# Log-sum-exp over heads on one core: 4 MB loads in place of 2 MB, bias parts taken as single rows by the first units, and factors made at the start of the late stages

## The chip, the cores and the metric

The kernel runs on one core of a Trainium2 chip. The metric is the device time of one execution in microseconds (us); the median of three executions of the kernel before is 326.98 us (326.78 to 327.11).

## The reference

`x` has 8 batches of 2048 rows with 2048 columns in float32; `bias` has 8 heads of 256 columns. Each row of `x` is cut into 8 heads, the head's bias is added, and the logarithm of the sum of exponentials is taken over the 256 columns. Every result is then written twice, for two neighbouring output rows.

```
x_heads = x.reshape(B, S, H, Dh).transpose(0, 2, 1, 3) + bias[None, :, None, :]
x_tiled = np.repeat(x_heads, 2, axis=2)
mx = x_tiled.max(axis=-1, keepdims=True)
lse = mx.squeeze(-1) + np.log(np.exp(x_tiled - mx).sum(axis=-1))
```

The kernel does without the maximum. It reads 134 MB of `x` and writes 1 MB.

## The kernel before

**Tiling.** A unit `t` is 256 rows of one batch: 128 partitions with K = 2 rows each, 2 MB. There are T = 64 units, eight to a batch. Nine buffers `xt` of 2 MB take them in turn (`NBUF = 9`). In the first seven batches a partition holds two neighbouring rows, one run of 16 KB in memory. The last batch (from unit 56) is laid out with consecutive rows on consecutive partitions. From unit 57 on a unit is loaded and worked on as single rows per partition (1 MB, `K` pieces), and unit 63 in still smaller pieces of columns (`LAST_COLS`). Below, (57,0) is the first row per partition of unit 57.

**The stages.** `STAGES` gives a split of the eight heads over the engines, by unit.

- Units 0 to 53 (`BULK`): heads 0 to 2 get their bias on the tensor engine (PE): three matmuls put the bias into PSUM (`put_bias`, L216), three more add `x` through an identity (`late_heads`, L275). The scalar engine (ACT) takes exp out of PSUM: head 0 with a running sum (L286), heads 1 and 2 back into the buffer (L293). Heads 4 to 7 get the bias from GpSimd (POOL) in place (`g_add`, L325). Then ACT takes exp of heads 3 to 7 (`later`, L331), the vector engine (DVE) multiplies head 3 by exp(bias) (L343) and adds up heads 1 to 7 in one reduction (L350).
- Units 54 to 56 (`MIXED`): head 0 goes over PE and ACT (`add_x` L251, `sum_biased` L306), heads 1 to 3 are exponentiated raw and weighed with exp(bias) on DVE (`weigh`, L366), heads 4 to 7 as in the bulk.
- From unit 57 on: single rows; POOL has no addition any more but folds one or two heads (`fold`, L382 and L390, with the rest on DVE at L396), DVE weighs the others.

**Factors and bias parts.** exp(bias) stands in `one_ps` (heads 1 and 2, PSUM), `w_ps` (heads 3 to 6, PSUM) and `w_sb` (heads 6 and 7). `one_ps` serves head 0 of the bulk as well, so its factors are made when unit 54 begins, behind unit 54's products on PE (`spread` L182, exp L500). The bias itself enters PE as three bfloat16 parts that add up to it: POOL makes them on one partition (`bparts`, L172 to L176), and three DMAs from POOL's queue put them on three partitions (`b3`, L178), so that one matmul with three rows adds all three.

**The order.** The program fixes the order by hand (`tc.manual_schedule`). In unit t's turn PE takes its products, POOL its addition, ACT and DVE do what was put off from unit t-1 (`for_pool`: exp of POOL's heads, the reduction), then ACT the heads of t. [...] The load of unit t + 9 is issued on SyncE's queue (SP, L143) after unit t's last step in program order, and waits for the last reads of the buffer. `on_x` keeps a list of who has touched a buffer, and drops those waits that follow from others.

**Results.** The sums of a batch stand in `R` (128 partitions x 2 rows x 8 heads x 8 blocks). `finish`, two units after a batch's end, turns them with two transposes on PE (L411) and takes Ln on ACT (L421, 64 partitions x 512). After unit 57 `store` writes seven batches at once (L425). `finish_last` does the same for the last batch (L432, L438, L439).

```
def load(t):
    after = last_uses[t - NBUF] if t >= NBUF else []
    for k0, k1, c0, c1 in pieces(t):
        loads[t, k0, c0] = on_x(t, nc.sync.dma_start(
            out=xts[t % NBUF][:, k0:k1, c0:c1], in_=rows_of(t)[:, k0:k1, c0:c1]), after)
```

Of the kernel before, what the change touches and what calls it, by code (L numbers as in the profile page):

```python
# [9 lines left out]
F32 = mybir.dt.float32  # L10
BF16 = mybir.dt.bfloat16
ACT = mybir.ActivationFunctionType
ALU = mybir.AluOpType


K = 2
NBUF = 9

NWARM = 3

# [29 lines left out]
def kernel(  # L50
# [6 lines left out]
    nc = tc.nc  # L57
    P = nc.NUM_PARTITIONS
    B, S, D = x.shape
    H, Dh = bias.shape  # L60
    assert D == H * Dh and S % (P * K) == 0
    NBLK = S // (P * K)
    T = B * NBLK
# [12 lines left out]
    brow = sb.tile([1, D], F32, name="brow")  # L76
    b_rep = sb.tile([P, D - G0], F32, name="b_rep")
    w_sb = sb.tile([P, D - W1], F32, name="w_sb")
    ident = sb.tile([P, P], F32, name="ident")
    ones = sb.tile([1, P], F32, name="ones")  # L80
    ones3 = sb.tile([3, P], BF16, name="ones3")
    b3 = sb.tile([3, CPE], BF16, name="b3")
    bparts = sb.tile([1, 3, CPE], BF16, name="bparts")
    brest = sb.tile([1, 2, CPE], F32, name="brest")

    R = [sb.tile([P, K, H, NBLK], F32, name=f"R{b}") for b in range(B - 1)]
    R_last = sb.tile([P, H, NBLK, K], F32, name="R_last")
    res = sb.tile([H * NBLK, B - 1, P, K, 2], F32, name="res")
    res_last = sb.tile([P, P, 2], F32, name="res_last")
    xts = [sb.tile([P, K, D], F32, name=f"xt{i}") for i in range(NBUF)]  # L90
    w_ps = pp.tile([P, W2 - W0], F32, name="w_ps")


    one_ps = pp.tile([P, MM], F32, name="one_ps")
    pairs = [pp.tile([P, 2 * MM], F32, name=f"pair{i}") for i in range(2)]
    ps = [p[:, c : c + MM] for p in pairs for c in (0, MM)]
    tpair = pp.tile([P, 2, K, P], F32, name="tpair")
    tps = [tpair[:, i] for i in range(2)]

    def modes_of(t):  # L100
        return [modes for t0, modes in STAGES if t0 <= t][-1]
# [1 line left out]
    def pieces(t):  # L103

        if len(modes_of(t)) == 1:
            return [(0, K, 0, D)]
        cols = [[(0, D)]] * K if t < T - 1 else LAST_COLS
        return [(k, k + 1, c0, c1) for k in range(K) for c0, c1 in cols[k]]

    def rows_of(t):  # L110

        b, blk = divmod(t, NBLK)
        v = x[b, blk * P * K : (blk + 1) * P * K, :]
        if b < B - 1:
            return v.rearrange("(p k) d -> p k d", k=K)
        return v.rearrange("(k p) d -> p k d", k=K)

    users = [[] for _ in range(T)]  # L120

    def on_x(t, ins, after):
        known = [u for u in users[t] if u.ins.engine != ins.ins.engine]
        for before in range(t % NBUF, t, NBUF):
            known += users[before]
        for u in known:
            if u not in after:
                tc.declare_no_dep(
                    ins.ins, u.ins, reason="waited for by those it waits for"
                )  # L130
        users[t].append(ins)
        return ins

    loads = {}

    last_uses = [[] for _ in range(T)]

    def load(t):
        after = last_uses[t - NBUF] if t >= NBUF else []
        for k0, k1, c0, c1 in pieces(t):  # L140
            loads[t, k0, c0] = on_x(
                t,
                nc.sync.dma_start(  # L143
                    out=xts[t % NBUF][:, k0:k1, c0:c1],
                    in_=rows_of(t)[:, k0:k1, c0:c1],
                ),
                after,
            )

    order = tc.manual_schedule()  # L150
    order.__enter__()
# [55 lines left out]
    def put_bias(m, k0, k1):  # L207

        if m["late"]:
            pair = pairs[n_ps[0] % 2]
            n_ps[0] += 1
            got = [one_ps, pair[:, 0:MM], pair[:, MM : 2 * MM]]
            for h, p in enumerate(got):
                nc.tensor.matmul(  # L216
                    p,
                    lhsT=ones3,
                    rhs=each_row(b3, h * Dh, Dh, K),
                    start=True,  # L220
                    stop=False,
                )
            return got + [pair]
        n = m["pe"] * Dh
        rows = min(k1 - k0, max(MM // n, 1))
        got = []
        for k in range(k0, k1, rows):
            for c in range(0, n, MM):
                w = min(n - c, MM)
                bank = n_ps[0] % len(ps)  # L230
                p = ps[bank][:, 0 : rows * w]
                n_ps[0] += 1
                mm = nc.tensor.matmul(
                    p,
                    lhsT=ones3,
                    rhs=each_row(b3, c, w, rows),
                    start=True,
                    stop=False,
                )
                on_bank(bank, mm)  # L240
                got.append((k, k + rows, c, w, bank, p))
        return got

    def add_x(m, t, k0, c0, c1, got):
# [3 lines left out]
        for ka, kb, c, w, bank, p in got:  # L248
            if not c0 <= c < c1:
# [14 lines left out]
    def keep_warm():  # L264
        for _ in range(NWARM):
            nc.tensor.matmul(  # L266
                tps[B % 2][:, 0], lhsT=ident, rhs=ident, start=True, stop=True
            )

    def late_heads(m, t, got, sums):  # L270
# [134 lines left out]

    def finish(b):

        nr = H * NBLK
        tp = tps[b % 2]
        for k in range(K):  # L410
            nc.tensor.transpose(  # L411
                out=tp[0:nr, k],
                in_=R[b][:, k].rearrange("p h n -> p (h n)"),
                identity=ident,
            )
        tv = bass.AP(
            tensor=tp.tensor,
            offset=tp.offset,
            ap=[[tp.ap[0][0], nr], [1, P], [P, K], [0, 2]],
        )  # L420
        nc.scalar.activation(out=res[:, b], in_=tv, func=ACT.Ln)  # L421

    def store():

        nc.sync.dma_start(  # L425
            out=out[0 : B - 1].rearrange("b h (n r) -> (h n) b r", n=NBLK),
            in_=res.rearrange("q b p k r -> q b (p k r)"),
        )

    def finish_last():  # L430
        tp = tps[(B - 1) % 2][:, 0]
        nc.tensor.transpose(  # L432
            out=tp, in_=R_last.rearrange("p h n k -> p (h n k)"), identity=ident
        )
        tv = bass.AP(
            tensor=tp.tensor, offset=tp.offset, ap=[tp.ap[0], [1, P], [0, 2]]
        )
        nc.scalar.activation(out=res_last, in_=tv, func=ACT.Ln)  # L438
        nc.sync.dma_start(  # L439
            out=out[B - 1].rearrange("h (n r) -> (h n) r", r=2 * P),  # L440
            in_=res_last.rearrange("q p r -> q (p r)"),
        )


    def sums_of(t):

        b, blk = divmod(t, NBLK)
        if b < B - 1:
            return R[b][:, :, :, blk]
        return R_last[:, :, blk, :].rearrange("p h k -> p k h")  # L450


# [6 lines left out]
        (modes_of(t)[k0], k0, k1)  # L459
        for t in range(T)  # L460
        for k0, k1, c0, _ in pieces(t)
# [9 lines left out]
    for t in range(T):  # L471
        xt = xts[t % NBUF]
        sums = sums_of(t)
        for k0, k1, c0, c1 in pieces(t):
# [62 lines left out]
        fb, at = divmod(t - 2, NBLK)  # L537
# [39 lines left out]
```

## Time and profile before

| what | value |
|---|---|
| median of three executions | 326.98 us |
| the profiled execution's own time | 327.16 us |
| its span in the trace | 325.4 us |
| granted tensor clock, mean of the span | 0.921 |
| PE busy | 263.2 us (81%) |
| DVE busy | 284.0 us (87%) |
| ACT busy | 264.7 us (81%) |
| POOL busy | 290.7 us (89%) |
| read from memory, mean rate | 134.23 MB, 416 GB/s |
| POOL's additions, L325 | 57, 4543 ns each |
| DVE's reductions in the bulk, L350 | 3.89 us each |

One execution was profiled; its times come from that execution. An idle time in square brackets is that of the engine just before the instruction, with what ended it. "x2" behind a shape merges neighbouring instructions of one line. In the table of stretches the columns are: the stretch, its length, the engine's busy time and number of instructions, the granted tensor clock, the DMA engines' share, and GB/s. In the slices of the span each digit or number stands for 8.1 us.

### The profile page before, as it was taken

The page shows a single profiled execution, that of the slowest core. Times are in us where ns is not written, and L with a number is a line of the kernel's source. Part 1 is how long each engine was busy: PE and PEld are TensorE (multiplying, and loading weights), DVE is VectorE, ACT ScalarE, POOL GpSimd, SP SyncE. Part 2 cuts the span into 40 slices and gives each one's busy share as a digit, 9 for nine tenths or more (in the row PEclk, how much of TensorE's full clock was granted, in tenths as well). Part 3 has the DMA queues.
Part 4 walks back from the last instruction along what each step waited for, and adds up shares of the span by engine and source line. Part 5 has one row for each costly group of instructions (what it writes and reads, how often), then busy time and mean ns, then how long its engine had stood idle before and what let it go on. Part 6 is the DMA issues. An engine that isn't in the chain of part 4 may idle for free.

```text
span 325.4 us, 2350 instructions
## 1 busy us (share of the span) xinstructions
PE 263.2 (81%) x649; PEld 98.6 (30%) x649; DVE 284.0 (87%) x306; ACT 264.7 (81%) x425; POOL 290.7 (89%) x123
## 2 busy tenths in 40 slices
PE   5398999599888789779779788887877897399984
PEld 2033333233323223223223223323223332044442
DVE  1008999999999999998998899989899799999985
ACT  1139999499969878987887969698788778889995
POOL 7999999899999999999999999999999899958874
PEclk9999999899979987997997979798998989569999
DMA  7999999999999999999999999999999999999995
GB/s 293 428 435 429 427 433 422 425 433 429 427 427 431 425 424 433 425 425 434 426 425 431 431 422 427 429 429 427 431 427 426 429 425 429 415 421 421 424 394 154
DMA packets 11934, 135.42 MB, mean 416 GB/s; under 512 B 1361, under 2 KB 1745, under 8 KB 2961
## 3 DMA queue, kind: packets, MB, share of 16 engines
q1 hardware_dynamic: 11824, 135.27, 98.9%
q8 instruction: 5, 0.08, 0.1%
q14 instruction: 7, 0.06, 0.0%
q0 software_dynamic: 96, 0.00, 0.0%
q10 hardware_dynamic: 2, 0.01, 0.0%
HBM read 134.23 MB, written 1.05 MB: 416 GB/s over the span
## 4 chain that ended last, share of the span: by engine, by line
DMA 48%; DVE 35%; POOL 6%; ACT 6%; PE 3%; issue 1%; SPq 0%; DVEq 0%
DMA xt<-in_x_dram 45%; DVE R L350 29%; ACT xt L331 5%; DVE xt L343 5%; POOL xt L325 4%; DMA b<-bparts 2%; PE pair L275 2%; DVE xt L366 2%; PE one_ps L275 1%; ACT xt L293 1%; DMA brow<-in_bias_dram 1%; POOL brest L173 1%; POOL brest L175 1%; PE pair L216 0%; POOL bparts L172 0%
## 5 line engine op out<-in xcount | busy, mean ns | idle before, releaser
L325 POOL TENSOR_TENSOR xt<-xt,b_rep 128x2048 f32<-128x2048 f32 x57 | 258.8, 4543 | 20.1 <-DMA xt<-in_x_dram 20.1
L350 DVE TENSOR_REDUCE R<-xt 128x14 f32<-128x3584 f32 (+1 forms) x56 | 214.5, 3831 | 1.9
L331 ACT ACTIVATE xt<-xt 128x2560 f32<-128x2560 f32 (+5 forms) x77 | 158.1, 2062 | 13.4 <-POOL xt L325 12.5
L275 PE MATMUL pair<-xt,ident 128*128 128x512 f32 x216 | 115.1, 660 | 0.0
L275 PE MATMUL one_ps<-xt,ident 128*128 128x512 f32 x108 | 66.7, 702 | 23.1 <-DMA xt<-in_x_dram 23.1
L293 ACT ACTIVATE xt<-pair 128x1024 f32<-128x1024 f32 x54 | 56.3, 1042 | 20.7 <-PE pair L275 19.3
L275 PEld LDWEIGHTS pair<-xt,ident 128*128 128x128 f32 x216 | 46.2, 214 | 61.5 <-issue 61.5
L343 DVE TENSOR_TENSOR xt<-xt,w_ps 128x512 f32<-128x512 f32 x54 | 36.8, 681 | 27.8 <-ACT xt L331 27.7
L286 ACT ACTIVATE xt<-one_ps 128x256 f32<-128x256 f32 x108 | 40.6, 391 | 7.9 <-PE one_ps L275 7.9
L216 PE MATMUL one_ps<-b,ones 3*128 3x512 bf16 x54 | 20.7, 383 | 18.4 <-ACT xt L286 12.4
L216 PEld LDWEIGHTS <-ones 3*128 3x128 bf16 x162 | 13.5, 92 | 70.2 <-issue 63.8
L216 PE MATMUL pair<-b,ones 3*128 3x512 bf16 x108 | 32.3, 378 | 0.0
L275 PEld LDWEIGHTS one_ps<-xt,ident 128*128 128x128 f32 x108 | 17.0, 198 | 46.4 <-DMA xt<-in_x_dram 39.6
L251 PE MATMUL pair<-xt,ident 128*128 128x512 f32 (+1 forms) x36 | 21.0, 669 | 7.2 <-DMA xt<-in_x_dram 7.1
L286 ACT ACTIVATION_READ_ACCUMULATOR xt<-one_ps 128x1 f32 x108 | 23.5, 218 | 0.0
L366 DVE CUSTOM_DVE_ANT_0 xt<-xt,w_ps 128x256 f32<-128x256 f32 x61 | 22.4, 419 | 0.0
L390 POOL TENSOR_TENSOR xt<-xt 128x128 f32<-128x128 f32 (+3 forms) x39 | 13.9, 356 | 3.1
L382 POOL TENSOR_TENSOR xt<-xt,w_sb 128x256 f32<-128x256 f32 (+1 forms) x13 | 10.1, 773 | 5.4 <-ACT xt L331 4.8
L266 PE MATMUL tpair<-ident 128*128 128x128 f32 x84 | 13.6, 300 | 0.5 <-ACT res L421 0.5
L306 ACT ACTIVATE xt<-pair 128x256 f32<-128x256 f32 x33 | 12.3, 387 | 0.0
L266 PEld LDWEIGHTS tpair<-ident 128*128 128x128 f32 x84 | 11.1, 200 | 4.1 <-issue 3.0
L366 DVE CUSTOM_DVE_ANT_0 xt<-xt,one_ps 128x256 f32<-128x256 f32 x27 | 10.6, 416 | 0.7 <-ACT xt L331 0.7
(40 smaller groups left out, 68.5 us busy)
## 6 DMA issues: line engine op xcount, KB each, us to landing
xt<-in_x_dram SPq DMA_DIRECT2D x57, 2048.0 KB, 30.8
xt<-in_x_dram SPq DMA_DIRECT2D x12, 1024.0 KB, 24.7
xt<-in_x_dram SPq DMA_DIRECT2D x4, 256.0 KB, 11.4
out_dram<-res SPq DMA_DIRECT2D x1, 896.0 KB, 6.6
xt<-in_x_dram SPq DMA_DIRECT2D x2, 384.0 KB, 16.0
xt<-in_x_dram SPq DMA_DIRECT2D x2, 128.0 KB, 6.3
out_dram<-res_last SPq DMA_DIRECT2D x1, 128.0 KB, 1.7
b<-bparts POOLq DMA_DIRECT2D x3, 1.5 KB, 6.4
```

The source lines that it names most:

```text
L216: nc.tensor.matmul(p, lhsT=ones3, rhs=each_row(b3, h * Dh, Dh, K), start=True, stop=False,)
L251: mm = nc.tensor.matmul(p, lhsT=ident, rhs=xts[t % NBUF][:, ka:kb, c : c + w], start=False, stop=True,)
L266: nc.tensor.matmul(tps[B % 2][:, 0], lhsT=ident, rhs=ident, start=True, stop=True)
L275: mm = nc.tensor.matmul(p, lhsT=ident, rhs=xts[t % NBUF][:, :, h * Dh : (h + 1) * Dh], start=False, stop=True,)
L286: act = nc.scalar.activation(out=xts[t % NBUF][:, k, 0:Dh], in_=got[0][:, k * Dh : (k + 1) * Dh], func=ACT.Exp, accum_out=sums[:, k, 0:1],)
L293: act = nc.scalar.activation(out=xts[t % NBUF][:, :, Dh : m["pe"] * Dh].rearrange("p k (h j) -> p h k j", j=Dh), in_=got[-1].rearrange("p ...
L325: add = nc.gpsimd.tensor_tensor(out=v, in0=v, in1=each_row(b_rep, c - G0, D - c, k1 - k0), op=ALU.add)
L331: return on_x(t, nc.scalar.activation(out=v, in_=v, func=ACT.Exp), [after])
L343: mul = nc.vector.tensor_tensor(out=f, in0=f, in1=each_row(w_ps, m["pe"] * Dh - W0, n, k1 - k0), op=ALU.mult,)
L350: red = nc.vector.tensor_reduce(out=sums[:, k0:k1, h0:H], in_=v.rearrange("p k (h j) -> p k h j", j=Dh), op=ALU.add, axis=mybir.AxisListTy ...
L366: ttr = nc.vector.tensor_tensor_reduce(out=v, in0=v, in1=w, scale=1.0, scalar=0.0, op0=ALU.mult, op1=ALU.add, accum_out=dst,)
L390: done = nc.gpsimd.tensor_tensor(out=v[:, :, 0:n], in0=v[:, :, 0:n], in1=v[:, :, n : 2 * n], op=ALU.add)
```

## The change

Four things change.

- **Loads.** A buffer is now a block `xb` of 4 MB, with KB = 4 neighbouring rows on a partition (one run of 32 KB in memory); there are four, so room for eight units (`NBUF = 8`). Units 0 and 1 are loaded each by itself into the first block. Units 2 to 55 are loaded as 27 blocks of two units with one DMA each; both units wait for that DMA. A block is loaded when both units of the block four before it have been read for the last time (`reload`, `load`). From unit 56 on loads are as before, but wait for the unit eight before instead of nine.
- **Results.** `R` and `res` follow the new rows: four columns of 32 rows in place of two of 64; `finish` makes four transposes, and Ln takes 32 partitions x 1024. One PSUM tile `tp` serves all batches.
- **Bias parts.** For the first five units (`NEARLY = 5`) `put_bias` takes the three parts from `bparts` where they are made, as three matmuls of one row each per bank, instead of one of three rows. The three DMAs that fill `b3` are issued from ACT's queue, ahead of its first exp, instead of POOL's.
- **Factors.** In the beginning only head 3's factors are made (256 columns of `w_ps`). The rest of `w_ps` (768 columns) and `w_sb` (512) are made by ACT from `b_rep` when unit 54 begins, behind the exp of `one_ps`.

```diff
-NBUF = 9
+KB = 4
+NBUF = 8
+NEARLY = 5
...
-    R = [sb.tile([P, K, H, NBLK], F32, name=f"R{b}") for b in range(B - 1)]
+    R = [sb.tile([P, KB, H, NB], F32, name=f"R{b}") for b in range(B - 1)]
...
-    xts = [sb.tile([P, K, D], F32, name=f"xt{i}") for i in range(NBUF)]
+    xbs = [sb.tile([P, KB, D], F32, name=f"xb{i}") for i in range(NBUF // TB)]
+    xts = [xb[:, k : k + K] for xb in xbs for k in range(0, KB, K)]
...
-    tpair = pp.tile([P, 2, K, P], F32, name="tpair")
-    tps = [tpair[:, i] for i in range(2)]
+    tp = pp.tile([P, KB, P], F32, name="tp")
...
-    def rows_of(t):
+    def rows_of(t, n=1):
-        b, blk = divmod(t, NBLK)
-        v = x[b, blk * P * K : (blk + 1) * P * K, :]
+        b, at = divmod(t, NBLK)
         if b < B - 1:
-            return v.rearrange("(p k) d -> p k d", k=K)
+            blk, i = divmod(at, TB)
+            v = x[b, blk * P * KB : (blk + 1) * P * KB, :]
+            return v.rearrange("(p k) d -> p k d", k=KB)[:, i * K : (i + n) * K]
+        v = x[b, at * P * K : (at + 1) * P * K, :]
         return v.rearrange("(k p) d -> p k d", k=K)
...
     def load(t):
+        if TB <= t < T - NBLK:
+            if t % TB == 0:
+                after = [u for i in range(TB) if t >= NBUF for u in last_uses[t + i - NBUF]]
+                ins = on_x(
+                    t,
+                    nc.sync.dma_start(
+                        out=xbs[t // TB % len(xbs)], in_=rows_of(t, TB)
+                    ),
+                    after,
+                )
+                for i in range(TB):
+                    loads[t + i, 0, 0] = ins
+            return
         after = last_uses[t - NBUF] if t >= NBUF else []
...
+    def reload(t):
+        n = t + NBUF
+        if n < T - NBLK:
+            if n % TB == TB - 1:
+                load(n - TB + 1)
+        elif n < T:
+            load(n)
...
     for i in range(3):
-        nc.gpsimd.dma_start(out=b3[i : i + 1, :], in_=bparts[:, i])
+        nc.scalar.dma_start(out=b3[i : i + 1, :], in_=bparts[:, i])
...
-    for c in range(W0, W2, MM):
-        spread(w_ps[:, c - W0 : c - W0 + MM], c, c + MM)
-    nc.scalar.activation(out=w_ps, in_=w_ps, func=ACT.Exp)
-    nc.scalar.activation(out=w_sb, in_=b_rep[:, W1 - G0 :], func=ACT.Exp)
+    w_late = w_ps[:, 0 : G0 - W0]
+    spread(w_late, W0, G0)
+    nc.scalar.activation(out=w_late, in_=w_late, func=ACT.Exp)
+
+    def prompt_factors():
+        spread(one_ps, V0, W0)
+        nc.scalar.activation(out=one_ps, in_=one_ps, func=ACT.Exp)
+        nc.scalar.activation(
+            out=w_ps[:, G0 - W0 :], in_=b_rep[:, 0 : W2 - G0], func=ACT.Exp
+        )
+        nc.scalar.activation(out=w_sb, in_=b_rep[:, W1 - G0 :], func=ACT.Exp)
...
             got = [one_ps, pair[:, 0:MM], pair[:, MM : 2 * MM]]
+            parts = [(ones3, b3)]
+            if n_ps[0] <= NEARLY:
+                parts = [(ones3[0:1], bparts[:, i]) for i in range(3)]
             for h, p in enumerate(got):
-                nc.tensor.matmul(
-                    p,
-                    lhsT=ones3,
-                    rhs=each_row(b3, h * Dh, Dh, K),
-                    start=True,
-                    stop=False,
-                )
+                for i, (lhsT, b) in enumerate(parts):
+                    nc.tensor.matmul(
+                        p,
+                        lhsT=lhsT,
+                        rhs=each_row(b, h * Dh, Dh, K),
+                        start=i == 0,
+                        stop=False,
+                    )
...
     def finish(b):
-        nr = H * NBLK
-        tp = tps[b % 2]
-        for k in range(K):
+        nr = H * NB
+        for k in range(KB):
             nc.tensor.transpose(
...
             if t == T_PROMPT and c0 == 0:
-                spread(one_ps, V0, W0)
-                nc.scalar.activation(out=one_ps, in_=one_ps, func=ACT.Exp)
+                prompt_factors()
...
-                if k1 == K and t + NBUF < T:
-                    load(t + NBUF)
+                if k1 == K:
+                    reload(t)
```

`on_x` is rewritten to match: it keeps its lists by block, and drops the waits between the two units of a block as well.

More of the change, by code (lines that the diff above doesn't have):

```diff
@@ L60 @@
     H, Dh = bias.shape
-    assert D == H * Dh and S % (P * K) == 0
+    assert D == H * Dh and S % (P * KB) == 0
     NBLK = S // (P * K)
+    NB = S // (P * KB)
+    TB = KB // K
     T = B * NBLK
@@ L84 @@
     brest = sb.tile([1, 2, CPE], F32, name="brest")
-    R = [sb.tile([P, K, H, NBLK], F32, name=f"R{b}") for b in range(B - 1)]
+    R = [sb.tile([P, KB, H, NB], F32, name=f"R{b}") for b in range(B - 1)]
     R_last = sb.tile([P, H, NBLK, K], F32, name="R_last")
-    res = sb.tile([H * NBLK, B - 1, P, K, 2], F32, name="res")
+    res = sb.tile([H * NB, B - 1, P, KB, 2], F32, name="res")
     res_last = sb.tile([P, P, 2], F32, name="res_last")
-    xts = [sb.tile([P, K, D], F32, name=f"xt{i}") for i in range(NBUF)]
+    xbs = [sb.tile([P, KB, D], F32, name=f"xb{i}") for i in range(NBUF // TB)]
+    xts = [xb[:, k : k + K] for xb in xbs for k in range(0, KB, K)]
     w_ps = pp.tile([P, W2 - W0], F32, name="w_ps")
@@ L108, in pieces @@
         return [(k, k + 1, c0, c1) for k in range(K) for c0, c1 in cols[k]]
-    def rows_of(t):
-        b, blk = divmod(t, NBLK)
-        v = x[b, blk * P * K : (blk + 1) * P * K, :]
+    def rows_of(t, n=1):
+        b, at = divmod(t, NBLK)
         if b < B - 1:
-            return v.rearrange("(p k) d -> p k d", k=K)
+            blk, i = divmod(at, TB)
+            v = x[b, blk * P * KB : (blk + 1) * P * KB, :]
+            return v.rearrange("(p k) d -> p k d", k=KB)[:, i * K : (i + n) * K]
+        v = x[b, at * P * K : (at + 1) * P * K, :]
         return v.rearrange("(k p) d -> p k d", k=K)
-    users = [[] for _ in range(T)]
+    users = [[] for _ in xbs]
     def on_x(t, ins, after):
[L123 to L127, printed above, removed]
+        buf = users[t // TB % len(xbs)]
+        for t_u, u in buf:
+            same = u.ins.engine == ins.ins.engine
+            if u not in after and (not same or t_u % NBUF == t % NBUF and t_u < t):
                 tc.declare_no_dep(
-                    ins.ins, u.ins, reason="waited for by those it waits for"
+                    ins.ins,
+                    u.ins,
+                    reason="another tile, or waited for by those it waits for",
                 )
-        users[t].append(ins)
+        buf.append((t, ins))
         return ins
@@ L266, in keep_warm @@
             nc.tensor.matmul(
-                tps[B % 2][:, 0], lhsT=ident, rhs=ident, start=True, stop=True
+                tp[:, 0], lhsT=ident, rhs=ident, start=True, stop=True
             )
@@ L418, in finish @@
             offset=tp.offset,
-            ap=[[tp.ap[0][0], nr], [1, P], [P, K], [0, 2]],
+            ap=[[tp.ap[0][0], nr], [1, P], [P, KB], [0, 2]],
         )
@@ L425, in store @@
         nc.sync.dma_start(
-            out=out[0 : B - 1].rearrange("b h (n r) -> (h n) b r", n=NBLK),
+            out=out[0 : B - 1].rearrange("b h (n r) -> (h n) b r", n=NB),
             in_=res.rearrange("q b p k r -> q b (p k r)"),
@@ L430, in finish_last @@
     def finish_last():
-        tp = tps[(B - 1) % 2][:, 0]
+        last = tp[:, KB - 1]
         nc.tensor.transpose(
-            out=tp, in_=R_last.rearrange("p h n k -> p (h n k)"), identity=ident
+            out=last, in_=R_last.rearrange("p h n k -> p (h n k)"), identity=ident
         )
         tv = bass.AP(
-            tensor=tp.tensor, offset=tp.offset, ap=[tp.ap[0], [1, P], [0, 2]]
+            tensor=last.tensor, offset=last.offset, ap=[last.ap[0], [1, P], [0, 2]]
         )
@@ L448, in sums_of @@
         if b < B - 1:
-            return R[b][:, :, :, blk]
+            return R[b][:, blk % TB * K :, :, blk // TB]
         return R_last[:, :, blk, :].rearrange("p h k -> p k h")
```

## The prediction

> **What bounds the kernel now.** I read first the page's slices, then the chain, then the timeline and the busy times of the end. A unit u is 256 rows (2 MB), a row unit (57,0) to (63,1) is 1 MB.
>
> ```profile
> DMA  7999999999999999999999999999999999999995
> GB/s 293 428 435 429 427 433 422 425 433 429 427 427 431 425 424 433 425 425 434 426 425 431 431 422 427 429 429 427 431 427 426 429 425 429 415 421 421 424 394 154
> xt<-in_x_dram SPq DMA_DIRECT2D x57, 2048.0 KB, 30.8
> ```
> The DMA engines are full from the second slice to the 38th, at about 428 GB/s in the bulk and 421 where single rows are loaded. A load lands 30.8 us after its issue, so some six wait in line: buffers are free in time.
>
> ```profile
> 289.12 4.66 ACT xt L331 x3
> 293.78 0.70 ACT xt L306 x4
> 294.48 20.15 DMA xt<-in_x_dram
> 314.63 0.02 issue
> 314.65 1.71 ACT xt L331
> 316.36 0.02 issue
> 316.38 0.42 DVE xt L366
> ```
> This is the end of the chain: the last landing in it is that of row (62,1) at 314.63; from there ACT and DVE run without a gap to the end. The chain's DVE share before 120 us is the backlog of a late start (first L343 at 25.86), worked off at 4.51 us a unit against 4.89 a landing; no transfer waited for it.
>
> ```profile
> 264.89 4.55 POOL L325 TENSOR_TENSOR xt<-xt,b_rep 128x2048 f32<-128x2048 f32 x1 [0.34 <-DMA xt<-in_x_dram]
> 269.79 4.55 POOL L325 TENSOR_TENSOR xt<-xt,b_rep 128x2048 f32<-128x2048 f32 x1 [0.35 <-DMA xt<-in_x_dram]
> 274.37 2.34 ACT L331 ACTIVATE xt<-xt 128x2560 f32<-128x2560 f32 x1 [0.70 <-POOL xt L325]
> 279.59 4.55 POOL L325 TENSOR_TENSOR xt<-xt,b_rep 128x2048 f32<-128x2048 f32 x1 [0.38 <-DMA xt<-in_x_dram]
> 284.17 3.29 ACT L331 ACTIVATE xt<-xt 128x2048 f32<-128x2048 f32 x2 [0.51 <-POOL xt L325]
> 289.12 4.66 ACT L331 ACTIVATE xt<-xt 128x2048 f32<-128x2048 f32 x3 [0.94 <-POOL xt L325]
> ```
> Units 52, 53, 55 on POOL: each starts 0.03 us after its landing, and ACT's exp of unit 53 waits for POOL's end. POOL needs 4.55 of every 4.89 us.
>
> ```profile
> 274.37:289.12 14.75, 12.95 (x19) 0.59 1.00 418
> 289.12:309.60 20.48, 20.48 (x44) 0.96 1.01 421
> 309.60:314.65 5.05, 4.64 (x11) 1.00 1.01 403
> 314.65:321.69 7.04, 7.04 (x20) 1.00 0.96 299
> ```
> ACT's busy time by stretch (length, busy): between 274.37 and 314.65 it is idle only 1.80 + 0 + 0.41 = 2.21 us. So the kernel is bound by DMA in the bulk and by ACT, just as tightly, in the last 40 us.
>
> [...] POOL starts after whole landings, 4.89 us apart. So the first unit of a 4 MB block can't start before the second has landed. [...] the slices reach 435. [...] ACT idles at 284.17 with later work in its queue. [...] The granted clock was 0.59 between 274 and 289; the two passes of one fp32 product (L251) took 1.13 us at 274.65 and 2.08 at 279.56.
>
> **The change, part by part.**
>
> *4 MB blocks, rate.* 27 blocks (units 2 to 55) take the place of 54 loads. Their cost isn't in the trace; I bound it by sizes that are. 2 MB landings are 4.89 us apart; 1 MB landings 2.49 (L251 on PE at 304.64, 307.13, 309.62). Two small ones cost 2 x 2.49 - 4.89 = 0.09 more than one twice the size. Whether that goes with the transfer or with the partition's contiguous run, both halve again: 27 x 0.09 = 2.4 us saved. Below: nothing, if 32 KB runs are cut into the 16 KB of now. [...] From 1 MB to 2 MB the rate only rose (421 to 428), so I leave a loss out. I take 2.0, since the row stage may be slow for other reasons too.
>
> *4 MB blocks, granularity.* Block (52,53) lands when unit 53 does now, 269.76. POOL, in order, adds unit 52 until 274.35 and unit 53 until 278.90; now 53 ends at 274.34. So ACT's exp of 53, now at 274.37, starts at 278.93: **4.56 us later**. POOL then has units 54 and 55 at 279.56 to 288.7, and 56 to 293.2 (now 289.1). Earlier in the run the same delay costs nothing: it frees buffers later, priced below. From 278.93 on ACT has to do all it does now in 274.37 to 314.65, 40.28 - 2.21 = 38.07 us busy, and what is added to it.
>
> *Factors made late.* In the head, exp of w_ps (1.01 us) and w_sb (0.62) and two spreads' worth of w_ps go; ACT waited 9.0 us there, so no gain. `prompt_factors` at unit 54 puts 768 and 512 columns on ACT: 0.74 (half of two 768-column exps, 316.97 to 318.44) + 0.52 = **1.26 us** in the full stretch. Its exp of one_ps waits for the spread on PE, which stands behind unit 54's product and so behind that block's landing at 279.56. Now, from PE's start to ACT's start it is 277.05 - 274.65 = 2.40 us with a warm clock: 281.96 here, while ACT is through with 53 at 281.2: 0.75 us idle. With a cold clock the product takes 0.95 more and the two spread passes about 0.7: 2.4 idle. [...] I take **1.5**.
>
> *Results in four columns.* `finish` transposes four times instead of twice (0.30 us each on PE, which idles) and its Ln takes 1024 columns instead of 512: 1.04 (L293, same size) - 0.59 = 0.45. Six lie in the bulk, where ACT has 4 us in 30 free; the seventh is in the tail: **0.45**. The 896 KB store issues at 315.36 and lands in 6.6 us, before the last output at 322.74; its runs double in length, no cost.
>
> *Sum for the tail.* Row (62,1)'s exp, at 314.65 now, starts at 278.93 + 38.07 + 1.26 + 0.45 + 1.5 = 320.2, 5.6 us later. Its data landed at 314.6, so what ends last is ACT; DVE needs 1.8 to 2.08 us a row against ACT's 2.09 and follows. From there ACT's 7.04 us to the end are the same. With landings 2.0 earlier: 5.6 - 2.0 = **+3.6**.
>
> *First units.* Five units get nine one-row matmuls instead of three: 30 more, at 0.25 us (three between 22.47 and 23.22) to 0.45 (three between 16.93 and 18.29[...]), 7.5 to 13.5 us of PE. They start when POOL ends the parts at 8.55, where now b3 is waited for until 16.90. Unit 0's products come some 6 us earlier, and by unit 5 PE waits for landings (33.1 for block 4,5). Gain at the end: none, as no transfer waits for this. If PE were late instead: the first reload needs unit 1 done, at about 28 us (unit 0's exps end near 19, then DVE twice 4.51), and the queue runs dry at 3.8 + 8 x 4.89 = 42.9, so 15 us cover it.
>
> *b3 by ACT's queue.* Three issues of about 0.5 us (bias load: 0.51) leave POOL (1.64 us there) and wait on ACT for POOL's parts until 8.55. Behind them on ACT stand exp of w_late and unit 0's heads, which need PE at about 13 at the earliest: cover. POOL adds unit 0 about 1.5 us earlier. Nothing at the end.
>
> *Eight buffers in four blocks.* SP's block load now waits for both units' last reads. A block lands at L; its second unit leaves POOL at L + 9.1, ACT at 11.4, DVE (0.60 + 3.89) at 16.1. The line holds out three blocks, 29.3 us: 13 us of cover, nothing lost. If it were gone, each microsecond late would be paid 27 times.
>
> Base: the profiled execution took 327.16 with a span of 325.4 (1.76 outside it), the median of the runs is 326.98. So 326.98 + 3.6 = **330.6**.
>
> **Rivals.** *Absorbed (faster):* the end is set by landings alone, as the chain says (314.63), and rows give back 2.49 - 2.09 = 0.40 us each. Then only the rate counts: 326.98 - 2.0 = 325.0. It decides if ACT's delay stays under the 0.4 us of idle it has at 309.6 to 314.65. Against: from 289.12 to 309.60 ACT is busy without a gap, so what rows can give back is spent already. 12%. *No faster transfer:* long runs are cut, 326.98 + 5.6 = 332.6. For: nothing shows a 32 KB packet. 15%. *Warm clock and more rate:* idle 0.75 instead of 1.5[...] 328.0, half of such outcomes within 0.2%. 13%. *Starved line:* blocks are freed too late; one microsecond on each of 27 gives 326.98 + 27 = 354. Cover speaks against it; 2%. The likeliest case, 329 to 332: 58%.
>
> **The numbers.** A change of under 0.2% (0.65 us) can't be told from none. Faster 0.12; within, 0.08 (half of the warm case); slower 0.80. The range goes from 327.2 (warm case's lower end) to 333.2 (no faster transfer, 332.6, and a little more cold clock); the likeliest case alone 329.0 to 332.0.
>
> **What would show it.** POOL's L372 in pairs back to back, a pair every 9.69 us or so; packets down by 27 x 128 and more (if they stay, the cut). Unit 56's add at about 286.7 instead of 284.55; ACT without a gap from about 281.5 on to the end, except before the exp of one_ps; the last 1792-column exp at 318 while its load landed at 312.6. Wrong if ACT waits for landings in the row stage, if POOL starts a block's first unit before the whole has landed, or if slices show gaps in DMA.

## The result, and the profile after

| | before | changed |
|---|---|---|
| median of the runs made side by side | 326.88 us (4 runs) | 329.9 us (329.29 to 331.01, 4 runs) |
| the profiled execution's own time | 327.16 us | 329.85 us |
| its span | 325.4 us | 327.7 us |

The ratio is 1.0096 [1.0068, 1.0124]: **slower by about 1%**, inside the predicted range and 0.7 us below the predicted 330.6. Of the 2.69 us between the two profiled executions, 2.3 lie in the span and 0.39 outside it (2.15 us now, 1.76 before).

The changed kernel's page, slices and loads, against the same rows of before:

```profile
DMA  8999999999999999999999999999999999999980
GB/s 313 456 432 408 440 447 432 408 440 444 436 408 438 444 429 416 436 444 429 416 436 439 428 420 436 444 428 420 436 442 424 425 432 408 422 423 418 411 306 16
DMA packets 7822, 135.42 MB, mean 413 GB/s; under 512 B 929, under 2 KB 1313, under 8 KB 2305
xb<-in_x_dram SPq DMA_DIRECT2D x27, 4096.0 KB, 22.1
```

The DMA engines are as full as before and reach the end of the loads sooner: in the 39th slice only 306 GB/s are moved, where it was 394. Single slices show up to 456 GB/s, where before the highest showed 435; over the interval of a block, 4 MB in 9.71 us, it is 432, and over that of a unit before, 2 MB in 4.89 us, it was 429. There are 7822 packets, where the page of before has 11934. The transfers did get faster, and the kernel still ends later. Two engines come late to the end. First the additions on GpSimd (start, duration, and in brackets the idle time before):

```profile
257.62 9.05 POOL L372 TENSOR_TENSOR xb<-xb,b_rep 128x2048 f32<-128x2048 f32 x2 [1.06 <-DMA xb<-in_x_dram]
267.33 9.07 POOL L372 TENSOR_TENSOR xb<-xb,b_rep 128x2048 f32<-128x2048 f32 x2 [0.66 <-DMA xb<-in_x_dram]
277.05 13.55 POOL L372 TENSOR_TENSOR xb<-xb,b_rep 128x2048 f32<-128x2048 f32 x3 [0.65 <-DMA xb<-in_x_dram]
```

Both units of a block are added back to back, a block every 9.71 us; in the whole execution GpSimd waits for the landings 27 times, once for each block. Unit 53 lies in the pair that starts at 267.33 and ends at 276.40; in the kernel before it ended at 274.34, although its data now lands earlier. Then ACT, around that point:

```profile
267.77 1.03 ACT L340 ACTIVATE xb<-pair 128x1024 f32<-128x1024 f32 x1 [1.51 <-PE pair L322]
...
276.43 2.34 ACT L378 ACTIVATE xb<-xb 128x2560 f32<-128x2560 f32 x1
279.43 0.58 ACT L230 ACTIVATE one_ps<-one_ps 128x512 f32<-128x512 f32 x1 [0.67 <-PE one_ps L217]
280.80 0.81 ACT L231 ACTIVATE w_ps<-b_rep 128x768 f32<-128x768 f32 x1 [0.78 <-DVE xb L390]
...
317.09 1.68 ACT L378 ACTIVATE xb<-xb 128x1792 f32<-128x1792 f32 x1
```

The second line is the exp of unit 53, 2.06 us later than before. It starts 0.03 us after GpSimd's end, but without a wait: since the first line, where ACT waited 1.51 us for PE's products of unit 51, it has worked without a gap, so here it came to unit 53 just as GpSimd was through. The next two lines make factors, each behind a wait. Left out are the exp of `w_sb` (281.55), that of unit 54 (282.07), the rows and the wider Ln (1.00 us at 297.19). The last line is the exp of row (62,1): 2.44 us later than the 314.65 of before. The busy times of two stretches (after the length come PE, its weight loads, DVE, ACT and POOL, each with its number of instructions; then the granted clock, the DMA share and GB/s):

```profile
290.60:317.09 26.49, 21.92 (x96) 11.85 (x95) 25.77 (x131) 26.49 (x58) 18.15 (x41) 0.93 1.02 408
317.09:324.13 7.04, 5.16 (x27) 3.05 (x26) 7.00 (x43) 6.99 (x22) 5.73 (x12) 1.00 0.13 45
```

Behind unit 56's addition ACT shows no wait: 26.49 us busy of 26.49, where the kernel before still had small waits for landings. The DMA share of 0.13 in the last stretch says that the loads were all but over. The chain that ended last says the same:

```profile
225.73 21.74 DMA xb<-in_x_dram
247.47 0.04 issue
247.52 2.08 PE one_ps L322 x2
...
267.77 1.03 ACT xb L340
268.79 2.23 ACT xb L378
...
280.17 0.60 DVE xb L390
280.78 0.02 issue
280.80 0.81 ACT w_ps L231
```

Before, a landing stood in the chain at 314.63. Now the last one is at 247.47; from there on the chain is work on PE, ACT and DVE alone, through the factor exps, to the end. GpSimd isn't in this last part.

### The profile page after: what moved, and what is told of

Same layout as the page of the kernel before. It is cut to its first block, busy times and chain, and to the rows that moved or that the text cites. A ratio compares the mean times of both kernels' runs of the same rounds, so it can differ in the third digit from the quotient of the medians.

```text
span 327.7 us, 2382 instructions
## 1 busy us (share of the span) xinstructions
PE 269.9 (82%) x691; PEld 102.7 (31%) x691; DVE 284.7 (87%) x306; ACT 266.7 (81%) x426; POOL 287.9 (88%) x120
## 2 busy tenths in 40 slices
DMA packets 7822, 135.42 MB, mean 413 GB/s; under 512 B 929, under 2 KB 1313, under 8 KB 2305
## 4 chain that ended last, share of the span: by engine, by line
DMA 41%; ACT 22%; DVE 16%; PE 16%; POOL 4%; issue 0%; SPq 0%; DVEq 0%
DMA xb<-in_x_dram 41%; ACT xb L378 15%; DVE R L397 12%; PE pair L322 6%; POOL xb L372 4%; PE one_ps L322 4%; ACT xb L353 3%; PE pair L263 2%; DVE xb L390 2%; ACT xb L340 2%; DVE xb L413 2%; PE one_ps L263 1%; PE pair L217 1%; ACT res L467 1%; ACT xb L333 1%; DMA brow<-in_bias_dram 1%
## 5 line engine op out<-in xcount | busy, mean ns | idle before, releaser
L372 POOL TENSOR_TENSOR xb<-xb,b_rep 128x2048 f32<-128x2048 f32 x57 | 257.6, 4541 | 24.1 <-DMA xb<-in_x_dram 24.1
L397 DVE TENSOR_REDUCE R<-xb 128x14 f32<-128x3584 f32 (+1 forms) x56 | 214.5, 3831 | 1.9
L378 ACT ACTIVATE xb<-xb 128x2560 f32<-128x2560 f32 (+5 forms) x77 | 156.9, 2048 | 13.0 <-POOL xb L372 13.0
L322 PE MATMUL pair<-xb,ident 128*128 128x512 f32 x216 | 114.7, 658 | 0.0
L322 PE MATMUL one_ps<-xb,ident 128*128 128x512 f32 x108 | 68.3, 717 | 16.5 <-DMA xb<-in_x_dram 16.5
L340 ACT ACTIVATE xb<-pair 128x1024 f32<-128x1024 f32 x54 | 55.4, 1026 | 25.6 <-PE pair L322 25.6
L322 PEld LDWEIGHTS pair<-xb,ident 128*128 128x128 f32 x216 | 46.3, 214 | 61.5 <-issue 61.5
L390 DVE TENSOR_TENSOR xb<-xb,w_ps 128x512 f32<-128x512 f32 x54 | 36.8, 682 | 30.1 <-ACT xb L378 30.0
L333 ACT ACTIVATE xb<-one_ps 128x256 f32<-128x256 f32 x108 | 39.8, 376 | 6.1 <-PE one_ps L322 6.1
L413 DVE CUSTOM_DVE_ANT_0 xb<-xb,w_ps 128x256 f32<-128x256 f32 x61 | 22.4, 418 | 0.0
```

What stands on the lines that cost most here:

```text
L322: mm = nc.tensor.matmul(p, lhsT=ident, rhs=xts[t % NBUF][:, :, h * Dh : (h + 1) * Dh], start=False, stop=True,)
L333: act = nc.scalar.activation(out=xts[t % NBUF][:, k, 0:Dh], in_=got[0][:, k * Dh : (k + 1) * Dh], func=ACT.Exp, accum_out=sums[:, k, 0:1],)
L340: act = nc.scalar.activation(out=xts[t % NBUF][:, :, Dh : m["pe"] * Dh].rearrange("p k (h j) -> p h k j", j=Dh), in_=got[-1].rearrange("p ...
L372: add = nc.gpsimd.tensor_tensor(out=v, in0=v, in1=each_row(b_rep, c - G0, D - c, k1 - k0), op=ALU.add)
L378: return on_x(t, nc.scalar.activation(out=v, in_=v, func=ACT.Exp), [after])
L390: mul = nc.vector.tensor_tensor(out=f, in0=f, in1=each_row(w_ps, m["pe"] * Dh - W0, n, k1 - k0), op=ALU.mult,)
```

## Experiments

The theory that the experiments started from: long runs make the transfers faster, but two units then arrive at once, the second is late on GpSimd by one addition, and ACT, which has no slack in the last 40 us, carries that lateness, the factors and the wider Ln to the end. The main rivals were: that the factors or the parts at the head cost the time, that the faster transfers come from the size of the transfer instead of the length of the run, and that blocks in themselves (buffers, layout) cost something.

Each edit is against the changed kernel. Times of before are from the runs beside each group: 326.77, 326.84 and 326.75 us. In the kernels with another end of the blocks the lines stand two further down (L374 for L372).

**Ending the blocks earlier.** One constant sets the unit from which loads are 2 MB again.

```diff
-        if TB <= t < T - NBLK:
+        if TB <= t < T_BLK:
...
-        if n < T - NBLK:
+        if n < T_BLK:
```

*T_BLK = 52.* 

> The changed kernel (329.9 us), but units 52 to 55 are loaded singly (2 MB each) again; 25 blocks of 4 MB stay. Backlog theory: POOL leaves the last 4 MB block's second unit 4.2 us late against its landing and works 4.55 us of every 4.89, so it makes good only 0.34 us a unit; four single units give back 1.4 us, less 2 x 0.07 for the slower loads: 328.6. Rival, only the last block's late landing counts: with the units single again the whole 4.5 us go, 325.5. Rival, the factors on ACT are the cost: no change, 329.9 to 330.

Measured: 329.25 us (328.38 to 329.88), ratio 1.0071 [1.005, 1.0093].

```profile
257.77 31.58 POOL L374 TENSOR_TENSOR xb<-xb,b_rep 128x2048 f32<-128x2048 f32 x7 [1.31 <-DMA xb<-in_x_dram]
```

The expectation of 328.6 was missed by 0.65. The seven additions from unit 50 on run without a gap: the backlog of one addition shrinks only by 4.89 - 4.51 = 0.38 us with each unit. Unit 56 ends 1.25 us earlier than in the changed kernel (289.35 against 290.60), and yet the exp of row (62,1) starts only 0.12 earlier (316.97). So it isn't the end of unit 56 that counts, as I had reckoned there, but how late ACT is at **unit 53**, whose exp moved from 276.43 to 276.26. The theory after that: with n units loaded singly up to unit 53, n times 0.35 to 0.38 is won back. The trace doesn't bear out that GpSimd alone carries it: here GpSimd ended unit 53 at 257.77 + 4 x 4.51 = 275.81, 0.59 earlier than in the changed kernel, and ACT, coming from an unbroken row of its own work since 267.65, reached it 0.45 after that.

*T_BLK = 46,* foretold with the theory so changed. 

> The changed kernel, but units 46 to 55 are loaded singly. The kernel with singles from 52 on took 329.25, that with singles from 40 on 325.31. Backlog theory, mended: ACT is full from unit 53 on, so what counts is how late POOL is at unit 53. A second unit of a block starts 4.53 us after its landing; each single unit after it makes good 0.35, eight of them 2.8, so 1.7 us are left at unit 53. 325.31 + 1.7 - 3 x 0.07 = 326.8. Rival, a threshold (POOL level or not at unit 56, where 4.5 - 11 x 0.35 = 0.7 is left): 325.5 to 326.

Measured: 326.8 us (326.42 to 327.01, 12 runs), ratio 0.9998 [0.999, 1.0007]. ACT's exp of unit 53 started at 273.41, that of row (62,1) at 314.03. The time was foretold to the tenth, with some luck: against T_BLK = 40 (272.33, next) unit 53 is 1.1 us late on ACT, not the 1.7 reckoned with. The rival of a threshold, 325.5 to 326, is out.

*T_BLK = 40.* 

> The changed kernel, but units 40 to 55 are loaded singly (2 MB); 19 blocks of 4 MB stay. Backlog theory: sixteen units give back 16 x 0.34 = 5.4 us, more than the 4.2 of the block, so POOL is level with the landings at unit 56; landings are some 2.0 us earlier than in the kernel before (2.5 less 8 x 0.07), and ACT's added 1.7 us go into the 2.2 us that it is idle there: 325.0. Rival, only the last block's landing counts: as the kernel with units 52 to 55 single, 325.5 to 326, and no difference between the two. Rival, the factors on ACT are the cost: 330.

Measured: **325.31 us** (325.06 to 326.62), ratio 0.9959 [0.9945, 0.9973].

```profile
282.50 4.55 POOL L374 TENSOR_TENSOR xb<-xb,b_rep 128x2048 f32<-128x2048 f32 x1 [0.42 <-DMA xb<-in_x_dram]
```

GpSimd waits for each landing again before the tail begins. ACT's exp of unit 53 starts at 272.33, 2.04 us before that of the kernel before, and that of row (62,1) at 312.63, 2.02 before. This version beats both kernels.

*T_BLK = 2,* no blocks at all, all else of the change kept. 

> The changed kernel with no 4 MB load at all: all units loaded singly, two rows of 16 KB runs from the new layout, eight buffers; head, factors and results as changed. Backlog theory: no backlog and no faster transfer: 326.9 + 0.1 for ACT = 327.0, landings 4.89 us apart. Rival, the factors and the wider Ln are the cost: 326.9 + 1.26 + 0.45 + 0.8 = 329.4. Rival, the wider stride or eight buffers cost: over 328 with gaps in the DMA slices.

Measured: 327.17 us (326.64 to 328.3, 20 runs), ratio 1.0017 [1.0009, 1.0026]. Landings are again 4.88 to 4.92 us apart by the starts on GpSimd, 239.55 to 283.90 (two are 5.06 and 4.97). Everything in the change but the 4 MB loads costs 0.4 us together, by a median of executions that spread over 1.7 us.

**What makes transfers faster.** The same 4 MB in one DMA, but with two runs of 16 KB on each partition (the two units' rows are taken from two places; the results then stand in other rows of the output):

```diff
-            return v.rearrange("(p k) d -> p k d", k=KB)[:, i * K : (i + n) * K]
+            v = v.rearrange("(i p k) d -> p i (k d)", i=TB, k=K)
+            return v[:, i : i + n]
```

> The changed kernel with 4 MB loads whose partitions take two runs of 16 KB (two rows each from the two halves of the block) in place of one of 32 KB; results of the first seven batches therefore stand in other rows than the reference has them. It parts the size of a transfer from the length of a run. If the cost goes with the run: blocks land 2 x 4.89 = 9.78 us apart, 27 x 0.07 = 1.9 us more than the changed kernel: 331.8. If it goes with the transfer: 9.71 as in the changed kernel, 329.9. Packets: 3456 more, if a packet is a run.

Measured: 331.9 us (331.75 to 332.71), ratio 1.0163 [1.0147, 1.0178]. GpSimd in this kernel, whose pairs start 9.79 us apart here and 9.71 in the changed kernel:

```profile
220.22 9.05 POOL L380 TENSOR_TENSOR xb<-xb,b_rep 128x2048 f32<-128x2048 f32 x2 [0.74 <-DMA xb<-in_x_dram]
230.01 9.05 POOL L380 TENSOR_TENSOR xb<-xb,b_rep 128x2048 f32<-128x2048 f32 x2 [0.74 <-DMA xb<-in_x_dram]
```

```profile
DMA packets 11278, 135.42 MB, mean 411 GB/s; under 512 B 929, under 2 KB 1313, under 8 KB 2305
```

Blocks land 9.79 us apart, as two loads of 2 MB did (2 x 4.89), and the packets are 11278 - 7822 = 3456 more, which is 27 x 128: one for each run that was cut. **The gain goes with the run, not with the size of the DMA.** This kernel has the lateness without the gain, and costs 2.0 us more than the changed kernel. As an estimate, one packet more costs 27 x 0.075 us x 16 engines / 3456 = 9.4 ns of one DMA engine.

*GpSimd or ACT.* In the nine profiles of this study whose blocks reach at least to unit 51, ACT starts unit 53's exp 0.03 to 0.45 us after GpSimd ends it. In four of them, as in the second profile of the changed kernel, ACT had stood waiting for GpSimd, 0.51 to 0.53 us:

```profile
276.40 2.34 ACT L378 ACTIVATE xb<-xb 128x2560 f32<-128x2560 f32 x1 [0.51 <-POOL xb L372]
```

In the other five it came out of its own work, which had waited for PE's products of unit 51. That the blocks make the end late, and by how much, is shown by the four ends of the blocks; that GpSimd's second addition is the only carrier is not. PE and ACT, too, get two units at once, and no run holds the one back without the other.

**The factors.** The two exps that `prompt_factors` added go back to the head, behind that of `w_late`:

```diff
     nc.scalar.activation(out=w_late, in_=w_late, func=ACT.Exp)
+    nc.scalar.activation(
+        out=w_ps[:, G0 - W0 :], in_=b_rep[:, 0 : W2 - G0], func=ACT.Exp
+    )
+    nc.scalar.activation(out=w_sb, in_=b_rep[:, W1 - G0 :], func=ACT.Exp)
```

> The changed kernel, but the 768 columns of w_ps and the 512 of w_sb are made in the head again (from b_rep, on ACT); only one_ps is made at unit 54. Backlog theory: ACT is full from unit 53 on, so all that it is spared shows: 1.26 of work and the 0.78 that it waited for DVE before writing w_ps, 2.0 in all: 327.9. Rival, the factors are the whole cost: 3 us less, 326.9 or under. Rival, ACT has room there and the landings decide: 329.9.

Measured: 329.0 us (328.6 to 329.75), ratio 1.0068 [1.0052, 1.0084]: 0.9 less than the changed kernel, where I expected 2.0. On ACT:

```profile
280.06 0.58 ACT L234 ACTIVATE one_ps<-one_ps 128x512 f32<-128x512 f32 x1 [1.28 <-PE one_ps L217]
...
290.71 3.28 ACT L378 ACTIVATE xb<-xb 128x2048 f32<-128x2048 f32 x2
```

Two things were missed. PE's spread was slower in this execution (1.60 us against 1.02), and ACT waited 1.28 us for it instead of 0.67. And with less work ACT meets the next hindrance: GpSimd ends unit 56 at 290.67, and ACT's exp of it starts at 290.71, where it was 291.93. More than 1.2 us couldn't be won there.

The same with T_BLK = 40: 

> Singles from unit 40 on and the 1280 columns of factors made in the head again. With singles from 40 on alone (325.31) ACT was full to the end, and the exp of row (62,1) started at 312.63, just when its load should land (314.63 before, less 2.0). Theory: landings are the floor there, so taking 1.26 us of work from ACT gains almost nothing: 325.0 to 325.3. Rival, ACT is the only bound: 324.0.

Measured: 325.54 us (325.09 to 325.63), ratio 0.9958 [0.9942, 0.9975], no gain over T_BLK = 40 alone. Behind the place where the work was taken away, ACT waits:

```profile
287.01 4.66 ACT L380 ACTIVATE xb<-xb 128x2048 f32<-128x2048 f32 x3 [0.51 <-POOL xb L374]
...
292.88 1.01 ACT L469 ACTIVATE res<-tp 32x1024 f32<-32x1024 f32 x1 [0.49 <-PE tp L459]
```

These two waits take up 1.0 of the 1.27 us of ACT's work. In this execution GpSimd starts on unit 56, behind its landing, at 282.43; PE's last transposes ahead of the Ln start at 292.24, the Ln follows at 292.88, and from there ACT has no wait again until the last results (320.44). With the blocks ended early, then, PE and ACT are about level there (waits of 0.5 us), and that much work on ACT costs nothing that shows.

*The order of the two exps.* The wait of 0.78 us ahead of `w_ps` came from DVE, which at that time still reads head 3's factors, other columns of the same tile (L390 of unit 53). With `w_sb` first, it should be covered:

```diff
         nc.scalar.activation(out=one_ps, in_=one_ps, func=ACT.Exp)
+        nc.scalar.activation(out=w_sb, in_=b_rep[:, W1 - G0 :], func=ACT.Exp)
         nc.scalar.activation(
             out=w_ps[:, G0 - W0 :], in_=b_rep[:, 0 : W2 - G0], func=ACT.Exp
         )
-        nc.scalar.activation(out=w_sb, in_=b_rep[:, W1 - G0 :], func=ACT.Exp)
```

> The changed kernel with the two added exps of the late factors in the other order: w_sb (0.52 us, waits for nothing) ahead of w_ps, which waited 0.78 us for DVE's multiplication of unit 53 to have read its part of w_ps. If that wait is on ACT's path, most of it is covered: 0.5 less than the changed kernel, 329.4, and the wait ahead of w_ps is down to 0.3. Rival, ACT waits elsewhere for what it gained here: no difference.

Measured: 329.44 us (328.86 to 330.85), ratio 1.0091 [1.0073, 1.0109].

```profile
280.92 0.81 ACT L232 ACTIVATE w_ps<-b_rep 128x768 f32<-128x768 f32 x1 [0.38 <-DVE xb L390]
```

The trace shows the wait halved, and ACT is 0.40 us earlier at unit 54's exp (281.67). The times can't tell: the intervals overlap.

*The changed kernel again,* beside these runs. 

> The changed kernel itself, beside the three others of this call on the same chip: 329.9, the measure for differences of half a microsecond.

Measured: 329.99 us (329.57 to 330.99), ratio 1.0105 [1.0089, 1.012]. Its profiled execution was as slow as the slowest, and shows one way in which single executions come to differ by more than a microsecond:

```profile
281.43 0.58 ACT L230 ACTIVATE one_ps<-one_ps 128x512 f32<-128x512 f32 x1 [2.69 <-PE one_ps L217]
```

The wait for PE's spread is 2.69 us instead of 0.67. GpSimd starts on block (54,55) at 277.04 and 277.05 in the two, so the landings agree; from there ACT gets the spread after 4.39 us here and 2.38 in the first profile, with a granted clock of 0.67 here and 0.86 there between 270 and 290. The second wait is gone (`w_ps` starts at 281.92), and row (62,1) starts at 318.19, 1.1 us later than in the first profile.

**The head.** Parts and DMAs of the beginning as they were:

```diff
-NEARLY = 5
+NEARLY = 0
...
-        nc.scalar.dma_start(out=b3[i : i + 1, :], in_=bparts[:, i])
+        nc.gpsimd.dma_start(out=b3[i : i + 1, :], in_=bparts[:, i])
```

> The changed kernel with the head of the kernel before: three-row bias matmuls from the first unit on, and b3 filled from POOL's queue. Theory: no transfer waits for the head, DVE's later start is worked off long before the end, so the same time as the changed kernel, 329.9, within 0.6. Rival, the one-row matmuls or ACT's DMA issues cost in the head: 0.5 to 1 us less. Rival, the early start brought a gain that the blocks hide: 1 to 5 us more, or a gap in the DMA slices at 40 us, as a 4 MB buffer is freed late. Outside the span (2.15 us in the changed kernel's profiled execution, 1.76 before): 1.76 if ACT's three DMAs make the difference.

Measured: 331.0 us (330.19 to 331.68), ratio 1.0129 [1.0108, 1.015]. Once more, beside the changed kernel: 

> The changed kernel with the head of the kernel before, once more beside the changed kernel; the first time it took 331.0 where 329.9 was expected, with intervals that overlap. Theory, nothing in the head reaches the end: the same as the changed kernel within 0.5. Rival, the later start of DVE (29.6 instead of 21.3) keeps DVE behind to the end: 1 us more again.

Measured: 331.16 us (330.15 to 332.63), ratio 1.0137 [1.0117, 1.0158], against 1.0105 [1.0089, 1.012]. I had expected no difference, and both times it was 1.1 to 1.2 us, though the intervals still touch. DVE's first step stands in the trace of the second of these kernels and of the changed one as:

```profile
30.05 0.69 DVE L390 TENSOR_TENSOR xb<-xb,w_ps 128x512 f32<-128x512 f32 x1 [21.81 <-ACT xb L378]
```

```profile
21.30 0.69 DVE L390 TENSOR_TENSOR xb<-xb,w_ps 128x512 f32<-128x512 f32 x1 [12.70 <-ACT xb L378]
```

So the head gives DVE 8.75 us. A part of that seems to reach the landings. The load of block (10,11) waits until DVE has read its buffer: in the changed kernel's first profile DVE ends unit 3's reduction at 40.39, and SP issues the load at 40.47. In its second profile DVE ends it at 43.50, and in the two where the head alone is undone at 47.80 and 48.20. In the three kernels with the old head and in four profiles with the new one, GpSimd starts on that block at 63.04 to 64.27 and at 62.73 to 63.03, and on block (54,55) at 277.24 to 277.95 and at 277.04 to 277.11, still 0.1 to 0.9 us apart. Why the later issue should cost, with the DMA engines busy all the while (a share of 0.97 or more in every ten us from 12 to 82 in the second of these two), and where the rest of the 1.1 us comes from, stays open.

*Blocks and results alone:* this head and the early factors together. 

> The head of the kernel before and all factors made there; of the change only the 4 MB blocks, the eight buffers and the four-column results stay. Theory, the blocks alone make the loss: with the factors early, as in the run without the head undone, 329.0, within 0.6, 2.2 above the kernel before. Rival, blocks and the other parts make it together: 327 to 328.

Measured: 329.88 us (328.71 to 330.37), ratio 1.0088 [1.0071, 1.0104]. The expectation, 329.0 within 0.6, was missed by 0.9: it had put the head at nothing, and the kernel with early factors and the new head took 329.0. The blocks, with the eight buffers and the four-column results that go with them, cost 3.1 us over the kernel before. That refutes the rival by which the factors make the loss: what they cost and what the head wins, about 1 us each, cancel.

## Why the prediction was right, step by step

**Rate: right, a little small.** 2.0 us were taken; block (54,55) landed at 277.05 against 279.59, **2.5 us** earlier. Of this 26 x (9.79 - 9.713) = 2.0 come from the intervals (9.713 is the mean of 14, from the start at 111.56 to that at 247.54; 9.79 is two of before), 0.3 from the first block, the rest from fewer irregular landings. In the three kernels with the old head it was 1.64 to 2.35 us earlier, so the loads by themselves gave about the 2.0, and the head the rest. The two carriers I left open are told apart: it is the run (9.71 us for 4 MB against 9.79 with the shorter runs). The rival without faster transfers is refuted with that. How far the rate could rise, in the rival with the warm clock, was my estimate; no trace showed it.

**Granularity: right in size, the carrier shown only in part.** Unit 53's exp was to start at 278.93 - 2.0 = 276.93, held back by GpSimd; it started at 276.43, by the 0.5 that the rate gave more, and GpSimd had ended the unit at 276.40. That ACT's own row, behind PE, would be as late was not in the prediction. The four ends of the blocks show the size: T_BLK of 56, 52, 46, 40 gave 329.9, 329.25, 326.8 and 325.31 us.

**Factors: the work right, the wait right by luck.** The two exps took 1.27 us (1.26 predicted). The waits sum to 0.67 + 0.78 = 1.45 against the 1.5 taken, but only 0.67 was for PE, near the 0.75 that I gave for a warm clock: the granted clock was 1.00 while unit 54's product ran, 1.12 us from 277.03 on. That the wait would lie about halfway to the 2.4 was my estimate. The 0.78 for DVE's reading of `w_ps` I had overlooked; it is 0.93 in both kernels with the head undone, where the wait for PE is 0.53, and absent in the changed kernel's second profile, where that wait is 2.69, above the 2.4 I gave as the slow end.

**Ln: right,** 0.42 for 0.45.

**The sum for the tail: 1.1 too high.** Row (62,1) was due at 320.2 - 2.0 = 318.2 and came at 317.09. Half is the faster rate, to which the head contributed. The other half is in the term of ACT's busy time, 38.07: I took stretch minus busy time for idle, 2.21 us. But in an unbroken row each record reaches about 0.1 us into the next (310.62 + 1.47 is 312.09, and the next starts at 311.99), so each wait is really about 0.1 longer than the columns show. With six waits in that stretch ACT had some 0.6 us more slack than I gave it. This reading is worked out from the records; no run was made for it.

**First units: wrong by about 1 us.** "Gain at the end: none" is the step that failed: undoing the head cost 1.1 to 1.2 us. My reason was that no transfer waits for it. With the old head DVE was through with unit 1, for which the first reload waits, only at 38.77 and 39.17 us in the two kernels with the head undone (30.76 and 32.22 in the two profiles of the changed kernel; in the first SP issued the load at 30.83). That is close to the 42.9 at which the prediction has the queue run dry, and later blocks landed late (block (10,11) by up to 1.5 us, by the starts on GpSimd).

**The base: wrong by 0.39.** The time outside the span went from 1.76 to 2.15 us. It is 2.11 to 2.22 in the profiled executions of all the kernels of this study, with the old head too, so ACT's DMA issues aren't the cause; it stays open. That the forecast of the time came within 0.7 us is in part luck: the tail was put too high by more than that, and this 0.39, which wasn't reckoned with, makes up for some of it.

**Eight buffers and the new layout: right.** Without blocks all the rest costs 0.4 us (T_BLK = 2), about what the time outside the span grew by. The rival by which landings alone set the end ("Absorbed") was to give 325.0 with all blocks; T_BLK = 40 comes near it with 325.31, once ACT and GpSimd have their slack back. Its chain has no landing after 262.77, though, so ACT is still as tight as the landings there.

## What to carry to other kernels

Here the 4 MB load gave its consumers two units at once (GpSimd's two additions, 9.05 us behind one landing), and the later one was done late by about one addition, 4.54 us, less what the rate won. With larger loads elsewhere ask how much slack the consumer has per unit (here 0.35 of 4.89 us on GpSimd) and end the large loads as many units ahead of a full stretch as it takes to win a step back (4.54 / 0.35 = 13 units, unit 40 for unit 53). If the rate is what is wanted, look at the length of a partition's run before the size of the DMA (4 MB took 9.71 us in runs of 32 KB, 9.79 in runs of 16 KB, as one DMA or two). When idle time is read from busy columns, add the overlap of the records for each wait (here about 0.1 us), and before putting work in a place that seems free look for who still reads the tile it writes (DVE here, a wait of 0.78 us).

## What the runs showed of the hardware

- Cutting each partition's run of 32 KB in two added one packet for each run (7822 to 11278) and cost, as an estimate, 9.4 ns of one DMA engine: 9.71 against 9.79 us for 4 MB, whether two DMAs of 2 MB or one of 4 MB carried the shorter runs.
- The small DMAs that bring the bias parts to `b3` (1.5 KB) took 5.6 us to land from ACT's queue in the changed kernel and 8.7 from GpSimd's with its head undone, beside the 4 MB loads, and 6.4 from GpSimd's beside the 2 MB loads of the kernel before.
- The same wait for PE's spread took 0.67 and 2.69 us in two executions of one kernel, with a mean granted clock of 0.86 and 0.67 between 270 and 290; the row (62,1) came 1.1 us later.
